# The first unit's splits, squares and measures in another order, a second bank for the given states, and identity products between the first turns

## The chip, the cores and the metric

The kernel runs on one core of a Trainium2 chip, in one launch. The metric is the device time of a launch in microseconds (us), lower is better; the kernel before has a median of 2393.8 us over three runs.

## The reference

One inference step of a decoder with two trunk layers, for a prompt of 2048 tokens and 8 given sequences with 4 new tokens each (32 sample tokens), width 1024. Layer 0 has four HGRN2 heads (A, 128 wide) and four forgetting-attention heads (B, with a paged cache), layer 1 four GLA heads (C, keys 128, values 256). Cut to what matters here:

```python
def even_mixer(h, ...):                    # h = rmsnorm(x, norm_even)
    qa, fa, ia, ga, qb, kb, vb, gb, fb = _split(h @ w_in, ...)
    f = lb + (1.0 - lb) * sigmoid(fa)
    o_a, s_a = gated_linear_chunked(ha(qa), ha(1 - f), ha(ia), ha(log(f)), hgrn_s0)
    ...
def gated_linear_chunked(q, k, v, log_f, s0):          # per chunk, also for the given states s0
    S_new = S * exp(b_last)[..., None] + einsum('bshk,bshv->bhkv', k * exp(b_last - b), v)
```

Layer 1 uses the same recurrence with values twice as wide.

## The kernel before

**Halves, units, turns.** The prompt goes through in two halves of 1024 tokens; the 32 sample tokens ride with the first half (`T` = 1056 columns there). `norm_groups` takes the half's tokens in groups of two tiles of 128 rows (the last group is the 32 sample rows). A group's `prep` loads its rows (`get_tile`, tiles nx_0, nx_128, ...), squares them on ScalarE with a row sum (L421), takes the root (VectorE L403, GpSimd L405) and scales them on VectorE (L423). Its `turn` transposes the rows on TensorE (tiles nt, two PSUM banks in turn) and evacuates each bank twice (`split_evac`): the high half of a two-term float16 on ScalarE (L465), the remainder on VectorE (L466).

**Weight units.** The projections come in units of 256 columns. `half_unit` gives four steps of a unit: 0 fetch (DMA, tile wr), 1 measure (VectorE: four maxima of a 128x512 part each, L292, and their maximum, L294, tile rm), 2 scale (a power of two from that maximum: TensorE spreads it over the partitions by an fp32 product with the identity, tiles spr, L279; VectorE L281, L270 to L272), 3 split (two float16 terms, tile w, in four parts). The parts alternate between two ways to split: scale and high term on ScalarE (L351, L352) with the remainder on GpSimd (L353), or high term on ScalarE (L345) with the remainder on VectorE (L346). Projections then take three matmuls for a k-tile (L470 to L472, high and low terms). The first units are Ai (values of HGRN2, tiles pt_Av; unit 0), Ag (gates, pf_Ag; unit 1) and two of Aqf (queries and forget gates of one head; units 2 and 3). Of the first unit, pS_Av are the sample tokens' projections (L514), for which VectorE copies their columns (sam_Av, L509).

**What sets the order.** Instructions are issued by hand-written generators (`handover`, `staged`, `mux`); `issue_after` sets a point for a block; a scheduler and pools of PSUM banks and tiles place the rest. Each engine takes its instructions in order. `staged` issues the later units' steps beside the running one, by a table `todo` of (unit, step) pairs. The first unit of a run has a table of its own, shown here:

```python
todo = [[(1, 0)], [], [(2, 0)], [(1, 1), (1, 2)], [(1, 3), (3, 0), (2, 1), (2, 2), (2, 3)]]
```

**Given states.** `lin_attn`'s `decode` computes the sample tokens' part of a linear head: for a group of given states sb (name s), TensorE computes keys times values (stS, L687), GpSimd multiplies the state by its decay (L689), VectorE adds the two (L691) and a DMA writes it out. The tile of stS has the PSUM tag "st", which has one bank; "gr" has two, used by transposes and the score products gl. Heads of layer 1 (value width 256) have two such groups in each half of the given states, heads of layer 0 one.

Of the kernel before, what the change touches and what calls it, by code (L numbers as in the profile page):

```python
# [8 lines left out]
F32 = mybir.dt.float32  # L9
# [112 lines left out]
class Kern:  # L122
# [134 lines left out]
    def spread(self, x, pps, tag, nm):  # L257

        nc = self.nc
        m, t = self.kcol(), self.kcol()  # L260
        nc.vector.tensor_reduce(m, x, mybir.AxisListType.X, ALU.max, apply_absolute_value=True)
        ps = pps.tile([P, 512], F32, tag=tag, name=f"spr_{nm}")
        nc.tensor.matmul(ps[:, :P], m.to_broadcast([P, P]), self.ident, start=True, stop=True)
        nc.vector.reduce_max(t, ps[:, :P], axis=mybir.AxisListType.X)
        return t

# [17 lines left out]
    def unit_scale(self, key, parts, rm, pool, pps, nm, undo, k):  # L284

        nc = self.nc

        def measure():
            if key in self.scales:
                return  # L290
            for a, r in enumerate(parts()):
                nc.vector.tensor_reduce(rm()[:, a : a + 1], r, mybir.AxisListType.XY, ALU.max,  # L292
                                        apply_absolute_value=True)
            nc.vector.reduce_max(rm()[:, WSPLIT:], rm()[:, :WSPLIT], axis=mybir.AxisListType.X)  # L294

        def scale():
            if key in self.scales:
                return
            sc = self.scales[key] = self.kcol(3)
            self.power(rm()[:, WSPLIT:], 2.0**14, sc, pool, pps, nm)  # L300
            if undo is not None:
                nc.vector.tensor_scalar(sc[:, 2:3], sc[:, 1:2], undo[:, 1:2], k, ALU.mult, ALU.mult)

        return measure, scale

# [9 lines left out]
    def half_unit(self, pool, pps, w, cols, key, nm, undo=None, k=1.0, also=(), raw=("wr", WU), lean=False):  # L315


        nc = self.nc
# [16 lines left out]
        def split():  # L335
            W = Parts(pool.tile([P, 2, KT, WU], F16, tag="w", name=f"w_{nm}"))
            s = self.scales[key][:, 0:1]
            for dst, inv in also:
                nc.vector.tensor_scalar(dst, self.scales[key][:, 1:2], inv[:, 1:2], None, ALU.mult)
            for a in range(WSPLIT):  # L340
                ks = slice(a * h, (a + 1) * h)
                r = t["raw"][:, ks, :width]
                hi, lo = (x[:, ks, :width] for x in W)
                if a % 2:
                    nc.scalar.activation(hi, r, AF.Copy, scale=s)  # L345
                    nc.vector.scalar_tensor_tensor(lo, r, s, hi, ALU.mult, ALU.subtract)  # L346
                    continue
                if lean:
                    nc.gpsimd.tensor_scalar(r, r, s, None, ALU.mult)
                else:  # L350
                    nc.scalar.activation(r, r, AF.Copy, scale=s)  # L351
                nc.scalar.activation(hi, r, AF.Copy)  # L352
                nc.gpsimd.tensor_tensor(lo, r, hi, ALU.subtract)  # L353
            return W
# [52 lines left out]

    def norm_groups(self, pool, pps, act, hf, get_tile, gain, tags=("gr", "o")):

        nc = self.nc  # L410
        tiles = self.ttiles(hf)

        def mk(grp):
            xs = []

            def prep():
                for c0, n in grp:
                    xt = get_tile(c0, n)
                    sq = pool.tile([P, D], BF16, tag="th", name=f"nsq{c0}")
                    ss = pool.tile([P, 1], F32, tag="nss", name=f"nss{c0}")  # L420
                    nc.scalar.activation(sq[:n], xt[:n], AF.Square, accum_out=ss[:n])  # L421
                    r = self.rstd(pool, ss[:n], [n, 1], D, f"n{c0}")
                    nc.vector.tensor_scalar(xt[:n], xt[:n], r, None, ALU.mult)  # L423
                    xs.append(xt)

            def turn():
                c0 = grp[0][0]
                if grp[-1][0] == HALF:
                    self.sam = None
                for k in range(KT):  # L430
                    ps = pps.tile([P, 512], F32, tag=tags[k % 2], name=f"nt{c0}_{k}")
                    w = 0
                    for (_, n), xn in zip(grp, xs):
                        nc.tensor.transpose(ps[:, w : w + n], xn[:n, k * P : (k + 1) * P], self.ident[:n, :n])
                        w += n
                    self.split_evac(ps[:, :w], act[0][:, k, c0 : c0 + w], act[1][:, k, c0 : c0 + w],
                                    gain[:, k : k + 1])

            return prep, turn

        return [mk(tiles[g : g + 2]) for g in range(0, len(tiles), 2)]

# [59 lines left out]
    def few_rows(self, pps, act, W, c0, nm, width):  # L502
# [3 lines left out]
        if self.sam is None:  # L506
            self.sam = self.few.tile([P, KT, 2, TS], act[0].dtype, tag="sam", name=f"sam_{nm}")
            for j, x in enumerate(act):
                nc.vector.tensor_copy(self.sam[:, :, j], as32(x[:, :, c0 : c0 + TS]))  # L509
# [21 lines left out]
    def lin_attn(self, wp, pps, hf, h, dv, q, f, k, v, vs, sg, gain, S, s0, s_out, p_out, ydst, nm):  # L531
# [107 lines left out]
        def decode():  # L639
# [31 lines left out]
            for half in range(2):  # L671
# [10 lines left out]
                yield 2.4 * dv  # L682
                for x, sb in enumerate(sbs):
                    b0 = 4 * half + x * cpb
                    st = pps.tile([P, cpb, dv], F32, tag="st", name=f"stS_{nm}{b0}")
                    for j in range(cpb):
                        nc.tensor.matmul(st[:, j], kpad[half][:, (b0 + j) % 4], v3, start=True, stop=True)  # L687
                    yield 213 * cpb
# [90 lines left out]
    def even_half(self, hf, act, wpool, wp, pps, npool, S):  # L779
# [7 lines left out]
            return wp.tile([P, HALF + TS], F32, tag="c4", name=nm)  # L787

        def unit(cols, nm, run, k=1.0):
            return (self.half_unit(wpool, pps, w, cols, nm, nm + str(hf), self.sx_even, k), run)  # L790

        def sc(nm):
            return self.scales[nm]
# [155 lines left out]
    def phase_even(self):  # L949
# [4 lines left out]
        with pool("act", side="right") as ap, pool("w", side="right") as w0, pool("wl", side="right") as wp1, \  # L954
# [5 lines left out]
            nrm = Pool(n0, {"th": 1, "nss": 4, "rs_t": 4, "rs_r": 4})  # L960
            self.scales2, self.ready, self.fsc, self.logit, self.v_undo = {}, {}, {}, {}, {}
            self.sx_even = self.gain_scale(self.g_even, pps, "pj", "e")
            S1 = sp.tile([P, P], F32, name="Sx")
            S = [(sp.tile([P, P], F32, name=f"S{h}"), S1) for h in range(NH)]
            act = self.alloc_act(ap)
# [19 lines left out]
            for hf in range(2):  # L985
# [12 lines left out]
                first = self.handover(groups, dense(0, 1), last)  # L998
                if hf == 0:
                    groups[0][0]()  # L1000
                    groups[0] = (lambda: None, groups[0][1])
                    for step in us[0][0]:
                        self.ready[0] = step()
                    drain(first)
                    with tc.issue_after(self.last_x.ins), tc.issue_after(self.last_a.ins), \
                            tc.issue_after(self.last_v.ins):
# [37 lines left out]
    def staged(self, us, a, b, beside=None):  # L1044
# [2 lines left out]

        def step(u, n):
            if u < len(us):
                self.ready[u] = us[u][0][n]()  # L1050

        for j in range(a, b):
            if j:
# [570 lines left out]
    def out_units(self, hf, layer, act, wpool, wp, pps, x2=None, done=None):  # L1624
# [4 lines left out]
        def mk(u):  # L1629
# [3 lines left out]
            def ev(ps, g, cnt, m):  # L1633
# [11 lines left out]
                else:  # L1645
                    for j in range(cnt):
# [4 lines left out]
                        if layer == 0 and u == 3:  # L1651
# [2 lines left out]
            return (self.half_unit(wpool, pps, w, [(u * 256, 256)], f"o{layer}{u}", f"o{layer}{hf}{u}",  # L1654
                                   also=list(zip(undo, (self.sy[layer], self.sy[2]))),
                                   raw=("yr", 256) if (hf, layer, u) == (0, 0, 0) else ("wr", WU),
                                   lean=(hf, layer, u) == (0, 0, 0)),
                    lambda W: self.proj_tm(pps, act, W, hf, ev, f"o{layer}{hf}{u}", pairs=not done or u < 3))

        return [mk(u) for u in range(4)]  # L1660
# [310 lines left out]
```

## Time and profile before

| what | value |
|---|---|
| three runs | 2399.18, 2390.87, 2393.8 us (median 2393.8) |
| profiled execution | 2395.09 us, span 2393.4 us, mean granted TensorE clock 0.987 |
| TensorE busy | 2294.6 us, 96% of the span |
| VectorE, ScalarE, GpSimd busy | 1414.6, 1108.6, 756.9 us |
| DMA | 317.24 MB, 133 GB/s on average |

Times in a row of a timeline are the start from the beginning of the span and the duration, in us; what stands in brackets is the idle time of the engine just before and what ended it. The rows of the list of waits give total, number and longest. A row of a window gives, after the window and its length, the busy time of TensorE, its weight loads, VectorE, ScalarE and GpSimd, the granted clock of TensorE (1 is full), the DMA share and GB/s. Matmuls overlap, so the distance of their starts says what one costs, not its duration. TensorE's `LDWEIGHTS` are counted apart.

### The profile page before, as it was taken

How to read it: one execution, taken by the hardware profiler on the slowest of the kernel's cores; microseconds unless marked ns; L12 is line 12 of the kernel's file. 1: busy time of each engine (PE TensorE's matmuls, PEld its weight loads, DVE VectorE, ACT ScalarE, POOL GpSimd, SP SyncE). 2: the span in 40 equal slices, each digit the busy share in tenths (PEclk: the TensorE clock that was granted, in tenths of full speed). 3: DMA queues.
4: the chain of work that ended last, by engine and by line, in shares of the span. 5: the costliest groups of instructions: out<-in, count | busy, mean ns of one | idle time of the engine just before them, and what ended most of it. 6: DMA issues, size and time to landing. Idle time of an engine off the chain costs nothing. (4 is left out here: it accounts for less than half of the span.)

```text
span 2393.4 us, 58665 instructions
## 1 busy us (share of the span) xinstructions
PE 2294.6 (96%) x23324; PEld 1635.2 (68%) x23324; DVE 1414.6 (59%) x3345; ACT 1108.6 (46%) x2460; POOL 756.9 (32%) x845
## 2 busy tenths in 40 slices
PE   7999999999999999999999999999999999999998
PEld 5667678854655876655446876777778766666887
DVE  7556556546664548567766463654675644557554
ACT  6434243343433126566676454535543635545333
POOL 2233323112212225234456211432452222322223
PEclk9999999999999999999999999999999999999999
DMA  6231235435431276776864632122156312115453
GB/s 182 79 87 58 85 119 161 147 108 148 147 116 59 82 217 214 254 250 200 264 223 155 191 109 63 50 82 85 44 156 193 107 42 69 43 59 159 154 190 150
DMA packets 297012, 317.24 MB, mean 133 GB/s; under 512 B 39729, under 2 KB 241010, under 8 KB 296738
## 3 DMA queue, kind: packets, MB, share of 16 engines
q1 hardware_dynamic: 295234, 308.98, 41.0%
q8 instruction: 183, 3.00, 0.5%
q0 software_dynamic: 1504, 4.52, 0.5%
q14 instruction: 91, 0.75, 0.1%
HBM read 242.31 MB, written 71.11 MB: 131 GB/s over the span
## 5 line engine op out<-in xcount | busy, mean ns | idle before, releaser
L472 PE MATMUL pt_o<-w_o,act 128*128 128x256 f16 x1024 | 280.4, 274 | 3.6 <-DVE act L1603 3.5
L470 PE MATMUL pt_o<-w_o,act 128*128 128x256 f16 x1024 | 280.7, 274 | 0.9 <-ACT sg1C L526 0.9
L471 PE MATMUL pt_o<-w_o,act 128*128 128x256 f16 x1024 | 280.4, 274 | 0.8 <-POOL w_o L353 0.8
L472 PEld LDWEIGHTS <-act 128*128 128x128 f16 x2304 | 226.3, 98 | 35.4 <-DVE act L1603 4.8
L470 PEld LDWEIGHTS <-act 128*128 128x128 f16 x2304 | 226.3, 98 | 35.2 <-ACT act L465 3.2
L471 PEld LDWEIGHTS <-act 128*128 128x128 f16 x2304 | 226.4, 98 | 31.6 <-issue 2.2
L470 PE MATMUL pt_Cv<-w_Cv,act 128*128 128x256 f16 (+1 forms) x512 | 140.4, 275 | 1.8 <-ACT act L465 1.0
L471 PE MATMUL pt_Cv<-w_Cv,act 128*128 128x256 f16 (+1 forms) x512 | 140.3, 275 | 0.0
L636 POOL TENSOR_TENSOR kA<-kA,fA 128x512 f32<-128x512 f32 (+1 forms) x56 | 79.5, 1421 | 191.5 <-PE gl_A L602 141.5
L472 PE MATMUL pt_Cv<-w_Cv,act 128*128 128x256 f16 (+1 forms) x512 | 140.0, 275 | 0.0
L1211 ACT ACTIVATE L<-L,nm,kc 128x512 f32<-128x512 f32 (+3 forms) x160 | 118.2, 741 | 37.8 <-DVE nm L1209 33.5
L636 POOL TENSOR_TENSOR kC<-kC,fC 128x512 f32<-128x512 f32 (+1 forms) x56 | 81.8, 1461 | 151.7 <-PE gl_C L602 107.2
L1219 POOL TENSOR_SCALAR L<-L,nm 128x512 f32<-128x512 f32 (+3 forms) x160 | 98.8, 631 | 63.3 <-DVE nm L1215 22.5
L1246 ACT ACTIVATE th<-pt 128x512 f16<-128x512 f32 (+3 forms) x159 | 80.7, 527 | 64.8 <-PE pt L1239 64.0
L1247 DVE TENSOR_TENSOR tl<-pt,th 128x512 f16<-128x512 f32 (+3 forms) x159 | 94.6, 608 | 23.3 <-ACT th L1246 22.3
L1239 PE MATMUL pt<-ident,L 128*128 128x128 f32 x544 | 92.7, 283 | 5.8 <-POOL L L1219 2.7
L1239 PEld LDWEIGHTS pt<-ident,L 128*128 128x128 f32 x544 | 68.0, 145 | 32.3 <-DVE tl L1247 8.7
L1363 PEld LDWEIGHTS pkt<-ident,pgcache_fox_k 128*128 128x128 f32 x512 | 58.4, 143 | 43.4 <-issue 25.9
L1363 PE MATMUL pkt<-ident,pgcache_fox_k 128*128 128x128 f32 x512 | 76.0, 281 | 7.3 <-DVE kts L1367 5.2
L470 PE MATMUL pt_Av<-w_Ai,act 128*128 128x256 f16 x256 | 70.2, 275 | 1.3 <-ACT act L465 1.3
L471 PE MATMUL pt_Av<-w_Ai,act 128*128 128x256 f16 x256 | 70.3, 275 | 0.8 <-POOL w_Ai L353 0.8
L472 PE MATMUL pt_Bk<-w_Bk,act 128*128 128x256 f16 x256 | 70.6, 276 | 0.0
(952 smaller groups left out, 6744.4 us busy)
## 6 DMA issues: line engine op xcount, KB each, us to landing
pgcache_fox_k<-in_cache_fox_k SPq DMA_DIRECT2D x128, 256.0 KB, 4.3
pgcache_fox_v<-in_cache_fox_v SPq DMA_DIRECT2D x128, 256.0 KB, 4.0
yr<-yT SPq DMA_DIRECT2D x16, 1024.0 KB, 6.6
nx<-in_x_prompt SPq DMA_DIRECT2D x16, 512.0 KB, 4.7
wr_Aqf<-in_w_in_even SPq DMA_DIRECT2D x64, 128.0 KB, 3.4
wr_o<-in_w_out_even SPq DMA_DIRECT2D x32, 256.0 KB, 4.2
wr_Cv<-in_w_in_odd SPq DMA_DIRECT2D x32, 256.0 KB, 4.1
wr_Cqk<-in_w_in_odd SPq DMA_DIRECT2D x64, 128.0 KB, 2.9
```

The costliest lines, as they stand in the source:

```text
L470: nc.tensor.matmul(ps, lh[0], rh[0], start=first, stop=False)
L471: nc.tensor.matmul(ps, lh[0], rh[1], start=False, stop=False)
L472: return nc.tensor.matmul(ps, lh[1], rh[0], start=False, stop=last)
L636: nc.gpsimd.tensor_tensor(kv[:, :, 0], kv[:, :, 0], t1.to_broadcast([P, nb, w]), ALU.mult)
L1211: self.last_exp = nc.scalar.activation(lt[:, :w], lt[:, :w], AF.Exp, bias=nm[:, 0:1], scale=ib, accum_out=nm[:, 2 + j : 3 + j])
L1219: nc.gpsimd.tensor_scalar(lt[:, :w], lt[:, :w], nm[:, 1:2], 2.0**14, ALU.mult, ALU.mult)
L1239: nc.tensor.transpose(pt[:, w : w + P], rows[b][s // 4][0][:, (s % 4) * P : (s % 4 + 1) * P], self.ident)
L1246: nc.scalar.activation(th[:, a:w], pt[:, a:w], AF.Copy),
L1247: nc.vector.tensor_tensor(tl[:, a:w], pt[:, a:w], th[:, a:w], ALU.subtract)))
L1363: nc.tensor.transpose(pk[:, j * P : (j + 1) * P], pgs[j][:, h * P : (h + 1) * P], self.ident)
```

## The change

Five parts:

1. The first unit (Ai, first half) splits all four parts as L345 and L346, high term on ScalarE and remainder on VectorE; before, two of four went through L351, L352 and L353. The flag `lean` of `half_unit` becomes `scaler` with the values None, "pool" and "vector".
2. The loads of the groups 1 and 2 of normalised rows are issued ahead; the squares and scalings of group 1 stand behind the last split of the first unit, of group 2 in the midst of group 1's turn, of group 3 behind that turn. Turns 1 and later follow.
3. Between the first turn's transposes TensorE gets 21 matmuls of the identity with itself into a bank (`warm`) that nothing reads: nine behind the first spread, four behind the first transpose, and one behind every transpose of the second tile.
4. The steps beside the first unit follow another table, and the measures of units 1 to 3 are issued after the last evacuation on VectorE at that point (`last_v`; the sample copies set it as well).
5. stS takes "st" and "gr" in turn for the groups of given states of one half.

```diff
-    def half_unit(..., raw=("wr", WU), lean=False):
+    def half_unit(..., raw=("wr", WU), scaler=None):
...
-                if a % 2:
-                    nc.scalar.activation(hi, r, AF.Copy, scale=s)
+                if a % 2 or scaler == "vector":
+                    self.last_split = nc.scalar.activation(hi, r, AF.Copy, scale=s)
                     nc.vector.scalar_tensor_tensor(lo, r, s, hi, ALU.mult, ALU.subtract)
                     continue
-                if lean:
+                if scaler == "pool":
...
+            def load():
+                raw.extend(get_tile(c0, n) for c0, n in grp)
             def prep():
-                for c0, n in grp:
-                    xt = get_tile(c0, n)
+                for j, (c0, n) in enumerate(grp):
+                    xt = raw[j] if raw else get_tile(c0, n)
...
-            def turn():
+            def turn(each=None):
...
+                            self.last_t = nc.tensor.transpose(...)
+                            if each:
+                                each(st, k, j)
...
             for j, x in enumerate(act):
-                nc.vector.tensor_copy(self.sam[:, :, j], as32(x[:, :, c0 : c0 + TS]))
+                self.last_v = nc.vector.tensor_copy(self.sam[:, :, j], as32(x[:, :, c0 : c0 + TS]))
...
-                    st = pps.tile([P, cpb, dv], F32, tag="st", name=f"stS_{nm}{b0}")
+                    st = pps.tile([P, cpb, dv], F32, tag=("st", "gr")[x % 2], name=f"stS_{nm}{b0}")
...
+            warm = pps.tile([P, 512], F32, tag="st", name="warm")
+            def warm_up(n, after):
+                with tc.issue_after(after.ins):
+                    for _ in range(n):
+                        nc.tensor.matmul(warm[:, :P], self.ident, self.ident, start=True, stop=True)
+            warm_up(9, self.last_spread)
...
                 if hf == 0:
                     groups[0][0]()
-                    groups[0] = (lambda: None, groups[0][1])
                     for step in us[0][0]:
                         self.ready[0] = step()
+                    for g in groups[1:3]:
+                        g[2]()
+                    def behind(ins, g):
+                        with tc.issue_after(ins.ins):
+                            groups[g][0]()
+                    def each0(st, k, j):
+                        if j or k == 0:
+                            warm_up(1 if j else 4, self.last_t)
+                        if (k, j) == (2, 0):
+                            st.enter_context(tc.issue_after(self.last_scale.ins))
+                    def turn0():
+                        groups[0][1](each0)
+                    def turn1():
+                        groups[1][1](lambda st, k, j: behind(self.last_a, 2) if (k, j) == (KT // 2, 0) else None)
+                        behind(self.last_a, 3)
+                    steps = [lambda: None, lambda: behind(self.last_split, 1), lambda: None, lambda: None, groups[4][0]]
+                    turns = [turn0, turn1] + [g[1] for g in groups[2:]]
+                    first = self.handover(list(zip(steps, turns)), dense(0, 1), last)
...
                 with ExitStack() as st:
+                    if beside and n == 1 and u < 4:
+                        st.enter_context(self.tc.issue_after(self.last_v.ins))
                     self.ready[u] = us[u][0][n]()
...
-                todo = [[(1, 0)], [], [(2, 0)], [(1, 1), (1, 2)], [(1, 3), (3, 0), (2, 1), (2, 2), (2, 3)]]
+                todo = [[(1, 0)], [(1, 1)], [(2, 0), (1, 2), (1, 3)], [(3, 0)], [(2, 1), (2, 2), (2, 3)]]
```

TensorE and VectorE at the end of the first unit. In the rows pS_Av are the sample tokens' products, spr_Aqf the spread of unit 2's maximum (rm_Aqf_717 before, rm_Aqf_737 after) and pf_Ag unit 1's products. TensorE before, in the midst of the pS_Av:

```order
L514 MATMUL pS_Av_665<-w_Ai_153,sam_Av_662 32x256
L279 MATMUL spr_Aqf_723<-ident,rm_Aqf_717 128x128
L514 LDWEIGHTS sam_Av_662
L514 MATMUL pS_Av_665<-w_Ai_153,sam_Av_662 32x256
L514 LDWEIGHTS sam_Av_662
```

TensorE after, at the end of the pS_Av:

```order
L522 MATMUL pS_Av_705<-w_Ai_163,sam_Av_702 32x256
L522 LDWEIGHTS sam_Av_702
L522 MATMUL pS_Av_705<-w_Ai_163,sam_Av_702 32x256
L279 MATMUL spr_Aqf_743<-ident,rm_Aqf_737 128x128
L478 LDWEIGHTS w_Ag_599
L478 MATMUL pf_Ag_869<-act,w_Ag_599 128x352
```

The spread moved from between the 8th and 9th pS_Av to behind the 24th, directly ahead of the first pf_Ag. VectorE before, where that maximum is taken (nt_7 is the first group's last bank, nt_0 to nt_2 the second group's):

```order
L466 SCALAR_TENSOR_TENSOR act<-nt_7_239,g_even,act 128x256
L292 TENSOR_REDUCE rm_Aqf_717<-wr_Aqf_556 128x1
L466 SCALAR_TENSOR_TENSOR act<-nt_0_264,g_even,act 128x256
L292 TENSOR_REDUCE rm_Aqf_717<-wr_Aqf_556 128x1
L423 TENSOR_SCALAR nx_512_184<-nx_512_184,rsr_n_191 128x1024
L294 TENSOR_REDUCE rm_Ag_648<-rm_Ag_648 128x1
L403 TENSOR_SCALAR rst_n_199<-nss_197 128x1
L292 TENSOR_REDUCE rm_Aqf_717<-wr_Aqf_556 128x1
L466 SCALAR_TENSOR_TENSOR act<-nt_1_269,g_even,act 128x256
L292 TENSOR_REDUCE rm_Aqf_717<-wr_Aqf_556 128x1
L466 SCALAR_TENSOR_TENSOR act<-nt_2_274,g_even,act 128x256
```

VectorE after, from the sample copies on (rm_Aqf_903 is unit 3's maximum, few_Av the sum of the pS_Av):

```order
L292 TENSOR_REDUCE rm_Aqf_737<-wr_Aqf_582 128x1 x4
L165 TENSOR_SCALAR g_hgrn<-g_hgrn 128x4
L165 TENSOR_SCALAR g_gla<-g_gla 128x8
L172 TENSOR_TENSOR lb<-lb 128x4
L191 MEMSET wgr 80x512
L213 CAST mdiag<-ident 128x128
L232 MEMSET scT_855 128x1024
L232 MEMSET scT_856 128x1024
L292 TENSOR_REDUCE rm_Aqf_903<-wr_Aqf_693 128x1 x4
L527 TENSOR_TENSOR few_Av_730<-few_Av_730,pS_Av_705 32x256
L210 CAST mlev_803<-mtmp 128x64
L294 TENSOR_REDUCE rm_Aqf_737<-rm_Aqf_737 128x1
```

The reductions of unit 2's maximum moved behind the two sample copies (the row ahead of these), and its last step L294 behind the memsets and unit 3's reductions.

ScalarE over the second group's evacuations (nsq are squares; the number in nx is the first token). Before:

```order
L465 ACTIVATE act<-nt_0_264,g_even 128x256
L421 ACTIVATE nsq_196,nss_197<-nx_640_194 128x1024
L465 ACTIVATE act<-nt_1_269,g_even 128x256
L465 ACTIVATE act<-nt_2_274,g_even 128x256
L421 ACTIVATE nsq_246,nss_247<-nx_768_244 128x1024
L465 ACTIVATE act<-nt_3_279,g_even 128x256
L465 ACTIVATE act<-nt_4_284,g_even 128x256
L421 ACTIVATE nsq_256,nss_257<-nx_896_254 128x1024
```

After:

```order
L426 ACTIVATE nsq_270,nss_271<-nx_512_176 128x1024
L473 ACTIVATE act<-nt_4_268,g_even 128x256
L473 ACTIVATE act<-nt_5_289,g_even 128x256
L426 ACTIVATE nsq_278,nss_279<-nx_640_178 128x1024
L473 ACTIVATE act<-nt_6_294,g_even 128x256
L473 ACTIVATE act<-nt_7_299,g_even 128x256
L426 ACTIVATE nsq_306,nss_307<-nx_768_304 128x1024
L426 ACTIVATE nsq_316,nss_317<-nx_896_314 128x1024
L426 ACTIVATE nsq_386,nss_387<-nx_1024_384 32x1024
L473 ACTIVATE act<-nt_0_394,g_even 128x256
```

The squares that stood between the second group's evacuations, one after each or two, came to stand later, the last three together ahead of the third group's first evacuation.

TensorE in the first C head's decode. Before, up to stS_C002 (the next pair, stS_C004, comes behind 89 further rows):

```order
L602 MATMUL gl_C_21886<-qC_21136,kC_21137 24x16 x32
L687 MATMUL stS_C_21929<-hl_C_21762,kpad_C_21771 128x256 x2
L471 LDWEIGHTS act
L471 MATMUL pt_Cv_21943<-w_Cv_21226,act 128x256
L472 LDWEIGHTS act
```

After, stS_C002 and stS_C004:

```order
L695 MATMUL stS_C_21949<-hl_C_21782,kpad_C_21791 128x256 x2
L479 LDWEIGHTS act
L479 MATMUL pt_Cv_21963<-w_Cv_21246,act 128x256
L480 LDWEIGHTS act
L480 MATMUL pt_Cv_21963<-w_Cv_21246,act 128x256
L478 LDWEIGHTS act
L478 MATMUL pt_Cv_21963<-w_Cv_21246,act 128x256
L479 LDWEIGHTS act
L479 MATMUL pt_Cv_21963<-w_Cv_21246,act 128x256
L480 LDWEIGHTS act
L480 MATMUL pt_Cv_21963<-w_Cv_21246,act 128x256
L695 MATMUL stS_C_22053<-hl_C_21782,kpad_C_21792 128x256 x2
```

The third pair, stS_C004, moved up to five pt_Cv matmuls behind the second.

More of the change, by code (lines that the diff above doesn't have):

```diff
@@ L262, in spread @@
         ps = pps.tile([P, 512], F32, tag=tag, name=f"spr_{nm}")
-        nc.tensor.matmul(ps[:, :P], m.to_broadcast([P, P]), self.ident, start=True, stop=True)
+        self.last_spread = nc.tensor.matmul(ps[:, :P], m.to_broadcast([P, P]), self.ident, start=True, stop=True)
         nc.vector.reduce_max(t, ps[:, :P], axis=mybir.AxisListType.X)
@@ L301, in scale @@
             if undo is not None:
-                nc.vector.tensor_scalar(sc[:, 2:3], sc[:, 1:2], undo[:, 1:2], k, ALU.mult, ALU.mult)
+                self.last_scale = nc.vector.tensor_scalar(sc[:, 2:3], sc[:, 1:2], undo[:, 1:2], k, ALU.mult, ALU.mult)
         return measure, scale
@@ L313, in sources, with half_unit @@
                 off += n
-    def half_unit(self, pool, pps, w, cols, key, nm, undo=None, k=1.0, also=(), raw=("wr", WU), lean=False):
+    def half_unit(self, pool, pps, w, cols, key, nm, undo=None, k=1.0, also=(), raw=("wr", WU), scaler=None):
         nc = self.nc
@@ L413, in mk @@
         def mk(grp):
-            xs = []
+            xs, raw = [], []
+            def load():
+                raw.extend(get_tile(c0, n) for c0, n in grp)
             def prep():
-                for c0, n in grp:
-                    xt = get_tile(c0, n)
+                for j, (c0, n) in enumerate(grp):
+                    xt = raw[j] if raw else get_tile(c0, n)
                     sq = pool.tile([P, D], BF16, tag="th", name=f"nsq{c0}")
@@ L429, in turn @@
                     self.sam = None
[L430 to L439, printed above, removed]
+                with ExitStack() as st:
+                    for k in range(KT):
+                        ps = pps.tile([P, 512], F32, tag=tags[k % 2], name=f"nt{c0}_{k}")
+                        w = 0
+                        for j, ((_, n), xn) in enumerate(zip(grp, xs)):
+                            self.last_t = nc.tensor.transpose(ps[:, w : w + n], xn[:n, k * P : (k + 1) * P], self.ident[:n, :n])
+                            w += n
+                            if each:
+                                each(st, k, j)
+                        self.split_evac(ps[:, :w], act[0][:, k, c0 : c0 + w], act[1][:, k, c0 : c0 + w],
+                                        gain[:, k : k + 1])
+            return prep, turn, load
         return [mk(tiles[g : g + 2]) for g in range(0, len(tiles), 2)]
@@ L789, in unit @@
         def unit(cols, nm, run, k=1.0):
-            return (self.half_unit(wpool, pps, w, cols, nm, nm + str(hf), self.sx_even, k), run)
+            return (self.half_unit(wpool, pps, w, cols, nm, nm + str(hf), self.sx_even, k,
+                                   scaler="vector" if (hf, nm) == (0, "Ai0") else None), run)
         def sc(nm):
@@ L1049, in step @@
             if u < len(us):
-                self.ready[u] = us[u][0][n]()
+                with ExitStack() as st:
+                    if beside and n == 1 and u < 4:
+                        st.enter_context(self.tc.issue_after(self.last_v.ins))
+                    self.ready[u] = us[u][0][n]()
         for j in range(a, b):
@@ L1656, in mk @@
                                    raw=("yr", 256) if (hf, layer, u) == (0, 0, 0) else ("wr", WU),
-                                   lean=(hf, layer, u) == (0, 0, 0)),
+                                   scaler="pool" if (hf, layer, u) == (0, 0, 0) else None),
                     lambda W: self.proj_tm(pps, act, W, hf, ev, f"o{layer}{hf}{u}", pairs=not done or u < 3))
```

## The prediction

> **What bounds the kernel now.** I read the page's busy shares first, then the waits of TensorE in the first 70 us and where the added bank acts, then the timelines of those places. The page:
>
> ```profile
> PE 2294.6 (96%) x23324; PEld 1635.2 (68%) x23324; DVE 1414.6 (59%) x3345; ACT 1108.6 (46%) x2460; POOL 756.9 (32%) x845
> PE   7999999999999999999999999999999999999998
> ```
>
> TensorE is busy for 96% of the span, with the first 60-us slice among its two emptiest. So work taken off VectorE, ScalarE or GpSimd is worth something only where TensorE stands still for it. TensorE's waits from 0 to 70 us, and behind the dots one row from 1500 to 1800 us (total, times, longest):
>
> ```profile
> PE nt L434 <- DVE nx L423: 5.5, 3, 3.7
> ...
> PE nt L434 <- DVE act L466: 2.8, 2, 2.2
> PE pf_Ag L470 <- ACT w_Ag L352: 1.5, 1, 1.5
> PE pS_Av L514 <- DVE sam_Av L509: 1.2, 1, 1.2
> PE pt_Av L471 <- POOL w_Ai L353: 0.8, 1, 0.8
> PE pf_Ag L470 <- DVE pow_Aqf L281: 0.8, 1, 0.8
> ...
> PE stS_C L687 <- DVE s_C L691: 6.5, 3, 2.2
> ```
>
> The change touches a start with some 13 us of waits in the rows shown and three waits of 2.2 us later. TensorE's timeline (start, duration):
>
> ```profile
> 19.80 0.39 PE L470 MATMUL pt_Av<-w_Ai,act 128*128 128x256 f16 x1
> 21.03 0.37 PE L471 MATMUL pt_Av<-w_Ai,act 128*128 128x256 f16 x1 [0.84 <-POOL w_Ai L353]
> ...
> 23.12 0.42 PE L470 MATMUL pt_Av<-w_Ai,act 128*128 128x256 f16 x1
> 23.33 0.42 PE L471 MATMUL pt_Av<-w_Ai,act 128*128 128x256 f16 x1
> ...
> 24.42 0.27 PE L472 MATMUL pt_Av<-w_Ai,act 128*128 128x256 f16 x1
> 24.53 0.27 PE L470 MATMUL pt_Av<-w_Ai,act 128*128 128x256 f16 x1
> ...
> 49.80 0.27 PE L472 MATMUL pt_Av<-w_Ai,act 128*128 128x256 f16 x1
> ...
> 51.93 0.49 PE L279 MATMUL spr_Aqf<-ident,rm_Aqf 128*128 128x128 f32 x2
> 52.34 0.62 PE L514 MATMUL pS_Av<-w_Ai,sam_Av 128*32 128x256 f16 x16
> 54.49 0.47 PE L470 MATMUL pf_Ag<-act,w_Ag 128*128 128x352 f16 x1 [1.53 <-ACT w_Ag L352]
> 56.08 0.45 PE L470 MATMUL pf_Ag<-act,w_Ag 128*128 128x352 f16 x1 [0.81 <-DVE pow_Aqf L281]
> ...
> 60.72 0.50 PE L471 MATMUL pf_Ag<-act,w_Ag 128*128 128x352 f16 x1
> 61.02 0.46 PE L472 MATMUL pf_Ag<-act,w_Ag 128*128 128x352 f16 x1
> 61.31 0.31 PE L470 MATMUL pf_Ag<-act,w_Ag 128*128 128x352 f16 x1
> 61.46 0.31 PE L471 MATMUL pf_Ag<-act,w_Ag 128*128 128x352 f16 x1
> ```
>
> Starts are 0.21 us apart at 23 us and 0.11 apart at 24.5: the matmuls ran at half clock at first. After the stops around 53 to 56 us the wider pf_Ag matmuls are 0.29 us apart until 61.31, then 0.15. VectorE beside it:
>
> ```profile
> 45.81 2.46 DVE L292 TENSOR_REDUCE rm_Aqf<-wr_Aqf 128x1 f32<-128x512 f32 x4
> ...
> 51.32 0.22 DVE L509 COPY sam_Av<-act 128x256 f16<-128x256 f16 x1
> ...
> 51.67 0.22 DVE L509 COPY sam_Av<-act 128x256 f16<-128x256 f16 x1
> 51.94 0.48 DVE L191 MEMSET wgr<- 80x512 f32 x1
> ...
> 53.74 0.91 DVE L232 MEMSET scT<- 128x1024 f32 x1 [0.16 <-issue]
> 54.57 0.10 DVE L173 TENSOR_TENSOR lb<-lb 128x4 f32<-128x4 f32 x1
> ...
> 58.13 0.41 DVE L519 TENSOR_TENSOR few_Av<-few_Av,pS_Av 32x256 f32<-32x256 f32 x1
> ```
>
> **The change, part by part.** Three terms carry the sum.
>
> *A, the first unit (start to the last pt_Av).* Removed: two scale activations on ScalarE and two subtractions on GpSimd; added: two combined multiply-subtracts on VectorE. The last split then no longer ends behind GpSimd's 0.84 us wait. With squares 256 and 384 out of the way, I put the first pt_Av about 3 us before the 21.03 at which the dense run starts. The identity products keep TensorE active among the first transposes; if they bring full clock before pt_Av, the some 13 matmuls up to 23.7 save 0.1 us each, 1.4 us. Together 4.5 us. The nine products stand where TensorE waited 3.7 us for nx anyway, and the other twelve stand between transposes whose evacuations set the pace; I cost them at nothing, and without that cover they would cost at most their own time, about 3 us for the nine.
>
> Against it stands the new order. ScalarE now runs five squares among and behind the evacuations of the second group and ahead of the third's, the last three without a break:
>
> ```profile
> 22.60 1.10 ACT L421 ACTIVATE nsq<-nx 128x1024 bf16<-128x1024 f32 x1
> 23.55 0.24 ACT L421 ACTIVATION_READ_ACCUMULATOR nsq<-nx 128x1 f32 x1
> ```
>
> A square with its read takes some 1.05 us, so three hold ScalarE for 3.1 us in which no bank is emptied, and a run of four L292 reductions (2.46 us) now stands among the fourth group's evacuations on VectorE. The two sum to 5.6 us, partly beside matmuls, against 4.5 won. I take A = 0, with ends -4.5 (all kept) and +1.5 (all of the 5.6 shows and 4.1 is won).
>
> *B, behind the first unit.* The measure of the third unit moves behind the sample copies. TensorE's queue then has spr_Aqf directly ahead of pf_Ag; before, its operand had been reduced half a unit earlier and it ran among the pS_Av matmuls without a wait. TensorE cannot pass it. VectorE does after the copies: four reductions 2.46, three small L165 and L172 rows 0.2 (they stood between the two copies), the memsets and the cast 2.63 (51.94 to 54.57), four more reductions 2.46, one few_Av add 0.35, and a cast and the final small reduction 0.1 each, like the small row L173: 8.3 us. From 51.89, the end of the copies before, that gives 60.2; spr_Aqf takes 0.5 (its row), so pf_Ag starts near 60.7. The pS_Av matmuls end at 52.96: a hole of over 7 us in place of 1.53 and 0.81.
>
> The gate's split of ScalarE and GpSimd now comes ahead of the copies, so those two waits vanish; nothing else covers the hole. Before, 20 pf_Ag matmuls had started by 61.31 and the other 28 of the 48 take 28 x 0.15 = 4.2: end 65.5. After, from 60.7, with half clock for 3.4 us (12 matmuls, then 36 x 0.15 = 5.4) they end at 69.5; with 6.8 us (23, then 25 x 0.15 = 3.8) at 71.3. So +4.0 to +5.8. The third unit's own split is next: its scale follows spr_Aqf behind four more reductions, so it may be late by up to 1 us. I take B = +5, with ends +3.5 (0.5 us of the chain hidden) and +7.
>
> The sizes 3.4 and 6.8 come from one row, whose eighth figure is the granted clock:
>
> ```profile
> 54.00:55.00 1.00, 0.51 (x2) 0.28 (x3) 1.00 (x3) 1.00 (x3) 0.48 (x1) 0.74 0.22 60
> ```
>
> A mean of 0.74 between full and half puts the switch near 54.5, and 54.5 to 61.31 is 6.8 us at half clock, with the second stop of 0.81 in it. A restart without a second stop may be shorter; I set half of 6.8 as its lower end. The Trainium skill, "TensorE: Matmul & The Clock Gate", section "The HAM clock gate", has a free-running window of about 3.4 us, of which one idle one halves the clock and one busy one restores it. By that rule a hole of 7 us always restarts cold, and the wait before full clock lies between one and two windows, which is what the two ends above are. The trace's 6.8 us are two such windows, so it agrees.
>
> *C, the second bank.* In layer 1 of the first half stS_C002 waits because its bank is read by the add of stS_C000:
>
> ```profile
> 1509.18 0.71 PE L602 MATMUL gl_C<-qC,kC 128*24 128x16 f32 x64
> 1512.07 0.79 PE L687 MATMUL stS_C<-hl_C,kpad_C 96*128 96x256 f32 x2 [2.19 <-DVE s_C L691]
> 1512.67 0.44 PE L471 MATMUL pt_Cv<-w_Cv,act 128*128 128x256 f16 x1
> ...
> 1510.03 1.27 DVE L708 TENSOR_TENSOR vp_C<-vC,vp_C 128x256 fp32r<-128x256 f32 x1
> 1511.33 0.69 DVE L691 TENSOR_TENSOR s_C<-s_C,stS_C 128x512 f32<-128x512 f32 x1
> ```
>
> With the other bank it does not wait, but in the new order stS_C004 follows only five matmuls later and needs the first bank, so the same add at 1511.33. The wait is then entered after stS_C002 (0.6) and five pt_Cv (0.6 to 1.1): 1.2 to 1.7 us per head stand under the wait instead of behind it. Three heads give -3.6 to -5. Part of it may go back where the later heads' work now meets its own operands. I take C = -2, nearer to nothing than to the full sum, since VectorE's order ahead of L691 has not become shorter; ends -6.5 (all three waits) and 0.
>
> The scheduler also shifts rows in the forgetting-attention part of layer 0 and nothing is added there; I take 0, with 2 us either way, the size of one wait of the kind seen above.
>
> Sum: 0 + 5 - 2 = +3 on the profiled 2395.1, so 2398. That execution lies 1.3 us above the median of the three runs, 2393.8; for a median I say 2397.
>
> **Rivals.** *A holds (faster).* If the evacuations behind the three squares are covered by the first group's 48 matmuls, all of A = -4.5 stays; with B at its low end +3.5 and C at -6.5 that is -7.5, 2386. The stretch from 25 to 50 us (busy time of TensorE, its loads, VectorE, ScalarE and GpSimd):
>
> ```profile
> 25.00:50.00 25.00, 24.93 (x220) 21.42 (x217) 18.25 (x49) 14.45 (x35) 3.87 (x6) 1.00 0.49 108
> ```
>
> For it: TensorE was the only engine without slack there, so 10 us of ScalarE could take the squares. Against: all three ends are needed at once, since from +3 it takes 10 us to a verdict of faster.
>
> *The hole costs more (slower).* One mechanism: TensorE stands for spr_Aqf, restarts at half clock for two steps, and finds the third unit's split late behind the four reductions that follow. B is then +7; if the C wait only moves (C = 0) and A is +1, the sum is +8, 2402. It decides when the end of the 48 pf_Ag moves past 72 us.
>
> *The second bank does not help.* stS_C004 takes over the whole wait, C = 0: 2399. This and the next stay within the bound.
>
> *The hole is not there*, because spr_Aqf's operand is reduced in time: B = -2, and the total is about -4, 2390. Against it stands the order of VectorE's queue.
>
> **How the numbers follow.** About 0.3%, 7.2 us, is what this kernel's runs can tell from no change. The forecast with C between its ends 0.45; second bank worthless 0.15; hole absent 0.06; the slower rival 0.24; the faster one 0.10. The first three are within the bound, but for a few hundredths at its edge; so faster 0.10, same 0.64, slower 0.26. The range 2389 to 2406 leaves out the full gain of A with C, and a hole that sets off further waits.
>
> **What would show it.** Right: the first pt_Av before 19 us with a short spacing; the last pt_Av again near 49 to 51 us; a wait of 6 to 7 us at spr_Aqf for L294 and pf_Ag matmuls 0.29 us apart behind it; the two waits of pf_Ag gone; the three waits of 2.2 us at stS_C about half as long and at stS_C004. Wrong: a last pt_Av near 45 us, a wait at spr_Aqf below 3 us, or half clock behind it for more than 7 us.

## The result

| kernel | runs | median | lowest to highest | to the kernel before |
|---|---|---|---|---|
| before | 6 | 2396.49 us | 2390.87 to 2399.99 | 1 |
| changed | 6 | 2407.39 us | 2405.05 to 2410.52 | 1.0052, 95% interval 1.0039 to 1.0065 |

The change makes the kernel slower by 0.52%, some 12 us (9 to 16 by the interval). The forecast was 2397 us, a change within 0.3%, with 2389 to 2406 as range: the time lies above it. The profiled execution of the changed kernel took 2405.05 us, and its page begins:

```profile
span 2403.3 us, 58746 instructions
...
PE 2295.2 (96%) x23366; PEld 1636.0 (68%) x23366; DVE 1421.3 (59%) x3347; ACT 1109.0 (46%) x2458; POOL 754.7 (31%) x843
```

TensorE's busy time differs from before by 0.6 us, the span by 9.9: the loss is standing still. Where it arises is found by pairing TensorE's matmuls of the two traces by output and count:

| matmul | before, us | changed, us | difference |
|---|---|---|---|
| pt_Av, 1st | 19.80 | 14.43 | -5.4 |
| pt_Av, 49th (second group) | 28.78 | 23.17 | -5.6 |
| pt_Av, 145th (fourth group) | 43.05 | 43.28 | +0.2 |
| pS_Av, 9th | 52.34 | 52.70 | +0.4 |
| pf_Ag, 17th | 60.14 | 65.01 | +4.9 |
| pt_Bk, 52nd | 368.15 | 370.31 | +2.2 |
| fo, 472nd (forgetting attention) | 1300.06 | 1298.50 | -1.6 |
| pt_o, 105th (output projection, layer 0) | 1319.21 | 1320.66 | +1.5 |
| pt_o, 205th | 1331.03 | 1340.50 | +9.5 |
| pf_C03q, 67th (fourth C head) | 1707.32 | 1718.12 | +10.8 |
| end of the span | 2393.4 | 2403.3 | +9.9 |

There are two jumps: 4.5 us at pf_Ag, which was forecast, and some 9 us between the 97th pt_o (1318.33 us before, difference -0.5) and the 219th (1333.47 us before, +8.7), at a place that the prediction never looked at. The slower drift between the two can't be read from single traces: before, e10 and e13 (below) have the same order on every engine up to 1315 us, and their 472nd fo start at 1300.06, 1294.33 and 1300.57 us. So only jumps within a short stretch are read here, or many traces together.

TensorE's waits up to 80 us, changed kernel:

```profile
PE spr_Aqf L279 <- DVE kc L261: 7.2, 1, 7.2
PE spr_e L263 <- DVE kc L261: 3.4, 1, 3.4
PE nt L440 <- DVE act L474: 1.9, 2, 1.2
PE pS_Av L522 <- DVE sam_Av L517: 1.7, 2, 1.5
PE pt_Av L478 <- ACT act L473: 0.9, 1, 0.9
PE nt L440 <- DVE nx L428: 0.7, 2, 0.4
```

The pf_Ag waits of before are gone and one of 7.2 us stands in their place (L261 is the row behind L294, and the two overlap at 60.4 to 60.5; in e1 and e9 the same wait is put down to rm_Aqf L294). The timelines of TensorE and, behind the dots, VectorE:

```profile
52.70 0.62 PE L522 MATMUL pS_Av<-w_Ai,sam_Av 128*32 128x256 f16 x16 [0.22 <-DVE sam_Av L517]
60.56 0.79 PE L279 MATMUL spr_Aqf<-ident,rm_Aqf 128*128 128x128 f32 x2 [7.24 <-DVE kc L261]
61.15 0.50 PE L478 MATMUL pf_Ag<-act,w_Ag 128*128 128x352 f16 x1
...
64.08 0.35 PE L479 MATMUL pf_Ag<-act,w_Ag 128*128 128x352 f16 x1
64.27 0.31 PE L480 MATMUL pf_Ag<-act,w_Ag 128*128 128x352 f16 x1
...
52.15 2.45 DVE L292 TENSOR_REDUCE rm_Aqf<-wr_Aqf 128x1 f32<-128x512 f32 x4
...
57.51 2.39 DVE L292 TENSOR_REDUCE rm_Aqf<-wr_Aqf 128x1 f32<-128x512 f32 x4
59.93 0.41 DVE L527 TENSOR_TENSOR few_Av<-few_Av,pS_Av 32x256 f32<-32x256 f32 x1
60.27 0.17 DVE L210 CAST mlev<-mtmp 128x64 int8<-128x64 f32 x1
60.37 0.14 DVE L294 TENSOR_REDUCE rm_Aqf<-rm_Aqf 128x1 f32<-128x4 f32 x1
```

From 52.15 to 60.37 VectorE runs the chain of the prediction, 8.2 us, and the pf_Ag matmuls start 0.29 us apart, half clock, from 61.15 to 64.1.

At the output projection TensorE waits (1300 to 1430 us, changed kernel; before had no wait for w_o L352 or sam_o here):

```profile
PE pt_o L478 <- ACT w_o L352: 3.9, 1, 3.9
PE pS_o L522 <- DVE sam_o L517: 1.7, 2, 1.5
...
PE pt_o L480 <- POOL act L1645: 0.8, 1, 0.8
PE pt_o L478 <- ACT act L1644: 0.8, 1, 0.8
...
PE pt_o L479 <- POOL w_o L353: 0.6, 1, 0.6
```

ScalarE and SyncE's queue say why. The first four rows are ScalarE and SyncE before, the next three ScalarE and SyncE of the changed kernel; yr is a piece of y on its way to `act` (four of 256 columns and a last one of 32), row are the residual rows:

```profile
1318.28 0.72 ACT L1602 ACTIVATE act<-yr,kc 128x512 f16<-128x512 f32 x1 [4.78 <-DMA yr<-yT]
...
1320.74 0.33 ACT L1602 ACTIVATE act<-yr,kc 128x64 f16<-128x64 f32 x1
...
1309.95 5.76 SPq L1589 DMA_DIRECT2D yr<-yT  x2
1315.82 5.82 SPq L1833 DMA_DIRECT2D row<-in_x_prompt  x8
...
1330.35 0.35 ACT L1647 ACTIVATE act<-yr,kc 128x64 f16<-128x64 f32 x1 [5.06 <-DMA yr<-yT]
...
1314.68 3.44 SPq L1878 DMA_DIRECT2D row<-in_x_prompt  x6
1321.74 0.38 SPq L1634 DMA_DIRECT2D yr<-yT  x1
```

The last piece is split 9.6 us later than before. Before, ScalarE stood 4.78 us for the piece ahead of it and not at all for this one; now it stands 5.06 us for this one, with the splits of the next unit's w_o behind it in its queue, and those are what TensorE waits for. The order of SyncE's queue tells it without a time: before, all yr pieces stood ahead of the nine rows; now the 32-column piece stands behind six.

```
before:   yr[128x8x256] yr[128x8x32] row_0 row_1 row_2 row_3 row_4 row_5 row_6 row_7 row_8
changed:  yr[128x8x256] row_0 row_1 row_2 row_3 row_4 row_5 yr[128x8x32] row_6 row_7 row_8
```

The edit contains nothing of this place. The scheduler that lays out the whole program came to another choice there; why it did is not shown.

### The profile page after: what moved, and what is told of

The parts are those of the page before. It is cut to its first block, busy times and chain, and to the rows that moved or that the text cites. A ratio compares the mean times of both kernels' runs of the same rounds, so it can differ in the third digit from the quotient of the medians.

```text
span 2403.3 us, 58746 instructions
## 1 busy us (share of the span) xinstructions
PE 2295.2 (96%) x23366; PEld 1636.0 (68%) x23366; DVE 1421.3 (59%) x3347; ACT 1109.0 (46%) x2458; POOL 754.7 (31%) x843
## 5 line engine op out<-in xcount | busy, mean ns | idle before, releaser
L1291 ACT ACTIVATE th<-pt 128x512 f16<-128x512 f32 (+3 forms) x159 | 81.0, 528 | 60.5 <-PE pt L1284 58.4
L478 PE MATMUL pt_Av<-w_Ai,act 128*128 128x256 f16 x256 | 70.6, 276 | 2.1 <-ACT act L473 2.1
L479 PE MATMUL pt_Av<-w_Ai,act 128*128 128x256 f16 x256 | 70.6, 276 | 0.6 <-DVE w_Ai L346 0.6
L480 PE MATMUL pt_Av<-w_Ai,act 128*128 128x256 f16 x256 | 70.5, 276 | 0.3 <-DVE act L474 0.2
```

Source lines behind the costliest of these rows:

```text
L478: nc.tensor.matmul(ps, lh[0], rh[0], start=first, stop=False)
L479: nc.tensor.matmul(ps, lh[0], rh[1], start=False, stop=False)
L480: return nc.tensor.matmul(ps, lh[1], rh[0], start=False, stop=last)
L1291: nc.scalar.activation(th[:, a:w], pt[:, a:w], AF.Copy),
```

## Experiments

Two theories were set against each other. Q: that one load's place in SyncE's queue costs most of the loss. H: the hole at spr_Aqf, with its restart, costs it all. Runs came in four lots with the kernel before beside them, whose medians were 2393.0 to 2393.7 us, so ratios are compared, not medians.

**e1**, the split undone: in `unit`, `scaler=None` for Ai0. By the order, this alone puts the short piece ahead again.

```diff
-    scaler="vector" if (hf, nm) == (0, "Ai0") else None
+    scaler=None
```

> The changed kernel, with the first unit split as before (two of four parts by ScalarE and GpSimd). VectorE's late maximum and with it the 7 us hole at spr_Aqf stays; in SyncE's queue the load of the last 32 columns of y (yr, 128x8x32) stands again ahead of all nine row loads of the output projection. Theory Q (queue: some 8 us of the 11 come from that load standing behind six row loads): 2396 to 2402 us, against 2407 for the changed kernel; the second jump near 1320 to 1330 us is gone, the hole of 7 us is there. Theory H (hole: the restart behind spr_Aqf carries the whole loss): 2405 to 2409.

Measured: 2398.39 us, ratio 1.0019 (1.0008 to 1.0030). The wait at spr_Aqf is 7.2 us as in the changed kernel, no wait for w_o stands at 1300 to 1345 us. Theory H, that the hole costs it all, falls.

**e2**, the measures freed:

```diff
-                    if beside and n == 1 and u < 4:
-                        st.enter_context(self.tc.issue_after(self.last_v.ins))
```

> The changed kernel, without the rule that puts the measures of units 1 to 3 behind the last evacuation. spr_Aqf stands among the pS_Av again, and SyncE's queue has the old order at the output projection. Theory Q: 2390 to 2396, both losses gone, by 11 to 17 us under the changed kernel. Theory H: the same, since the hole is gone as well. It bounds what the rest of the change is worth; no wait over 2 us at spr_Aqf.

Measured: 2396.31 us, ratio 1.0005 (0.9991 to 1.0019): no hole, no late piece, and no gain either.

**e3**, both edits:

> The changed kernel with both edits: split as before, measures without the rule. No hole at spr_Aqf, but SyncE's queue has the short load of y behind six row loads, as the changed kernel has. Theory Q: 2400 to 2406, a jump of 6 to 10 us near 1320 to 1340. Theory H: 2390 to 2397.

Measured: 2399.50 us, ratio 1.0033 (1.0019 to 1.0047). No hole, but the late piece, and slower than before; the time lies between the ranges of the two theories, at the edge of Q's.

**e4**, the kernel before with the vector split alone (`if a % 2 or vec:`, `vec` for Ai0 of the first half):

> The kernel before, with one part of the change alone: the first unit's four parts split by ScalarE and VectorE. No hole at spr_Aqf; SyncE's queue has the short load of y behind six row loads. Theory Q: 2400 to 2406, slower than before by 4 to 10 us though the start is not slower. Theory H: 2394 to 2397, within 1 us of the kernel before.

Measured: 2397.35 us, ratio 1.0020 (1.0006 to 1.0035): less than Q expected, and just above H's range. In its trace the third pf_Ag starts at 51.60 us (56.08 before), 4.5 us ahead; the 219th pt_o at 1342.26 (1333.47), 8.8 us behind. So the start is ahead with these splits, and the jump at the load that moves with them is larger than that. What the splits alone would be worth in the time is not shown: in e6, with rows held back, they win nothing over e10.

**e5**, the changed kernel with every row load of both output projections held behind the last load of y:

```diff
+                self.last_yr = nc.sync.dma_start(t["raw"], y[...])
...
+                    with self.tc.issue_after(self.last_yr.ins):
                         nc.sync.dma_start(t[:m], self.rows(hf, c0, m, first))
```

> The changed kernel, in which the nine row loads of the output projection are issued only after the last load of y, so that the 32-column piece stands ahead of them in SyncE's queue; the start with its hole is as in the changed kernel. Theory Q (the piece behind six row loads costs some 6 to 8 us): 2398 to 2402 us, 5 to 9 us below the changed kernel, and w_o's wait of 3.9 us on TensorE is gone. Theory R (the loss there comes from the other shifted rows of ScalarE and GpSimd, not from this load): 2405 to 2409. The state loads s_C move ahead of the piece too; if these hold it up, the wait stays under Q as well.

Measured: 2394.57 us, ratio 0.9998 (0.9984 to 1.0011), better than Q said. Against the changed kernel its trace gains 6 us between 1316 and 1474 us, and over 10 us from 2200 us on, where the same edit holds back rows of layer 1's last projection. The edit did two things, so e9 and e10 take them apart.

**e6**, e4 with the same edit:

> The kernel before, with the vector split of the first unit alone, and the row loads behind the last load of y. No hole and no late piece. Theory Q: 2389 to 2394, 4 to 8 us below the vector split alone (2397.4) and perhaps faster than the kernel before, since that run's trace was 4.5 us ahead of before at 56 us. Theory R: 2396 to 2399.

Measured: 2388.00 us, ratio 0.9973 (0.9963 to 0.9984), a little below Q's range, with the same double effect as e5.

**e7** and **e8**, the second bank added to before, and taken from the changed kernel (`tag=("st", "gr")[x % 2]` against `tag="st"`):

> The kernel before with the second bank for stS alone. The forecast had -2 us; the trace of the changed kernel shows stS_C004 3 to 4 us earlier in each head and the next head's products back where they were. Theory G (given back): 2392 to 2396, within 1 us of before. Theory C (the wait was worth 1.2 to 1.7 us per head): 2389 to 2391.

> The changed kernel with one bank for stS as before; the hole and the late piece stay. Theory G: within 1 us of the changed kernel, 2405 to 2408. Theory C: 2 to 5 us slower, 2409 to 2413.

Measured: e7 2390.02 us, ratio 0.9982 (0.9973 to 0.9990); e8 2407.51 us, ratio 1.0051 (1.0033 to 1.0069). So alone it looks worth 4 us, in the changed kernel nothing. TensorE in e7, waits of 1500 to 1800 us and two rows:

```profile
PE gl_C L602 <- issue: 4.1, 3, 1.5
PE stS_C L687 <- DVE s_C L691: 3.6, 3, 1.2
...
1513.24 0.51 PE L687 MATMUL stS_C<-hl_C,kpad_C 96*128 96x256 f32 x2 [1.21 <-DVE s_C L691]
...
1527.24 0.69 PE L602 MATMUL gl_C<-qC,kC 128*64 128x64 f32 x16 [1.21 <-issue]
```

The wait of 2.19 became 1.21 at stS_C004, as forecast, and another of 1.21 us came at the next gl_C of each head: 6.5 us of three waits became 3.6 and 4.1. Over the whole stretch of these heads, from the first oS_C (1502 us before) to the 40th pf_C03k (1720 us), e7 takes 215.4 us and before 218.0, so 2.6 us are won there, though the two spans are the same (2393.4); the changed kernel takes 216.9 and e8 216.1, so there nothing is won.

**e9**, e5's edit at the first output projection alone:

> The changed kernel, in which only the first output projection's row loads (layer 0, first half) wait in the order for the last load of y; the run before also held the row loads of layer 1's last projection back, whose trace gained 6 us after 2300 us. Theory Q (the late piece alone cost 6 to 8 us): 2398 to 2402 us. Theory L (the gain of the run before came from the last projection alone): 2404 to 2408.

Measured: 2401.51 us, ratio 1.0030 (1.0016 to 1.0044): 0.0022, 5 us, below the changed kernel. In the trace the wait for w_o is gone, and a new one of 3.1 us for the rows, now late themselves, has come; so the edit takes away only a part of the loss there.

**e10**, the edit in the kernel before, where it moves rows of the last projection only:

> The kernel before with the row loads behind the last load of y; in SyncE's queue the first projection keeps its order and only layer 1's last projection changes. Theory L': its row loads stood ahead of the loads of y there and cost 5 to 6 us: 2387 to 2390. If the gain in the trace was chance of that run: 2392 to 2396.

Measured: 2384.63 us, ratio 0.9963 (0.9951 to 0.9975). That is a gain of 9 us, more than expected, beside the question and of the same kind: rows that stood among the loads of y. From 2190 us on the waits before were, first three rows, and in e10, last row:

```profile
PE pt_o L472 <- DVE act L1603: 3.5, 2, 2.5
PE gl_C L602 <- DVE sam_o L509: 2.0, 1, 2.0
PE pt_o L470 <- ACT sg1C L526: 0.9, 1, 0.9
...
PE gl_C L602 <- DVE qC L635: 1.2, 1, 1.2
```

**e11**, e6 with the second bank:

> The kernel before with three edits: vector split of the first unit, row loads behind the last load of y, second bank for stS. No hole, no late piece. From 2388.0 for the first two and -3.4 for the bank alone: 2384 to 2386 if the bank's gain adds, 2387 to 2389 if it is given back as in the changed kernel.

Measured: 2386.45 us, ratio 0.9971 (0.9958 to 0.9985): the bank adds nothing to e6.

**e12**, the changed kernel without the 21 identity products; by the order the short piece is ahead again:

> The changed kernel without the 21 identity products. The hole stays, SyncE's queue has the old order. If they warm the clock: matmuls of the first unit start 0.2 us apart instead of 0.11 for some 15 matmuls, 1.4 us later at the first group's end, though the later waits for evacuations may take it back; time as with the split undone, 2396 to 2401. If they do nothing, the first pt_Av are 0.11 us apart here as well.

Measured: 2394.53 us, ratio 1.0004 (0.9992 to 1.0016), less than expected. The hole of 7.2 us is there and the jump at 1330 us is not. The first unit's matmuls, e12 and, behind the dots, the changed kernel:

```profile
17.14 0.42 PE L480 MATMUL pt_Av<-w_Ai,act 128*128 128x256 f16 x1
17.36 0.42 PE L478 MATMUL pt_Av<-w_Ai,act 128*128 128x256 f16 x1
...
17.13 0.27 PE L480 MATMUL pt_Av<-w_Ai,act 128*128 128x256 f16 x1
17.24 0.27 PE L478 MATMUL pt_Av<-w_Ai,act 128*128 128x256 f16 x1
```

The products do bring full clock early, and 2.3 us at the 46th pt_Av. By the 95th it is -1.0 us: there this execution of the changed kernel has lost its clock again. Even where it has not, in the traces of e5 and e8 (same start), the ninth pS_Av comes at 51.97 and 51.64 us, and in e12 at 51.52: at the end of the unit nothing is left of the products' gain.

**e13**, the clean one: the kernel before with the short piece's load placed behind the sixth row (its steps are issued in the loop over the rows, after `issue_after` of row 5). TensorE's and GpSimd's order is that of before, SyncE's differs in this load alone, and a few rows of ScalarE and VectorE follow it.

> The kernel before with one load moved: the 32-column piece of y is issued behind the sixth row load of layer 0's output projection, as the changed kernel has it; TensorE's and GpSimd's order is that of before, row for row, and the start is untouched. Theory Q: 2398 to 2403 us, with pt_o waiting 3.5 to 4 us for w_o near 1330 us and some 8 us lost there. Theory R (the load is a bystander, the other shifted rows cost the time): 2392 to 2395.

Measured: 2401.33 us, ratio 1.0027 (1.0012 to 1.0042), 6.5 us slower. ScalarE, SyncE, the window of the DMA engines (its last two figures are their busy share and GB/s) and TensorE:

```profile
1329.14 0.35 ACT L1602 ACTIVATE act<-yr,kc 128x64 f16<-128x64 f32 x1 [5.07 <-DMA yr<-yT]
...
1312.97 4.18 SPq L1835 DMA_DIRECT2D row<-in_x_prompt  x6
1317.68 0.38 SPq L1589 DMA_DIRECT2D yr<-yT  x1
...
1318.00:1329.00 11.00, 11.00 (x104) 9.85 (x102) 4.23 (x8) 3.60 (x6) 2.27 (x2) 1.00 1.05 380
...
PE pt_o L470 <- ACT w_o L352: 4.0, 1, 4.0
PE pt_o L471 <- POOL w_o L353: 0.6, 1, 0.6
```

The load is issued some 2 us later than in before, but its split starts 8.4 us later: six rows of 512 KB, 3.1 MB, go through the full DMA engines ahead of its 128 KB, and at 380 GB/s they take 8.3 us. In the trace they land in the order of their issue, some 1.25 us apart (first, second, fourth and fifth at 1321.7, 1322.9, 1325.4 and 1326.7 us), and the piece follows them, as in the changed kernel, where the sixth row lands at 1329.4 us and the piece at 1330.3. TensorE's difference to before goes from 1.3 us at the 500th fo (1305.50) to 8.8 us at the 219th pt_o (1333.47).

**e14**, e10 with the second bank:

> The kernel before with the row loads behind the last load of y (alone 2384.6 us) and the second bank for stS (alone 2390.0, 3.4 below before). If both add: 2380 to 2383; if the bank's gain was chance of that chip or is given back: 2384 to 2387.

Measured: 2384.09 us, ratio 0.9964 (0.9953 to 0.9976). It beats before and the changed kernel, by the row loads; the bank adds nothing that these times can tell.

Set out by the two suspects (ratios to before):

| | short piece ahead | short piece behind six rows |
|---|---|---|
| no hole at spr_Aqf | before 1; e2 1.0005; e7 0.9982 | e13 1.0027; e4 1.0020; e3 1.0033 |
| hole of 7.2 us | e12 1.0004; e1 1.0019 | changed 1.0052; e8 1.0051 |

The right column is above the left in every pairing: 0.0027 (e13 to before), 0.0033 (changed to e1), 0.0048 (changed to e12). The lower row is above the upper unevenly, by 0 (e12 to e2) to 0.0037 (e1 to e7), and other edits differ in these pairs as well.

The traces say the same place by place. From the 500th fo to the 219th pt_o, the five with the short piece behind six rows (changed, e3, e4, e8, e13) take 35.5 to 40.1 us. The seven with it ahead and the rows behind it as before (before, e1, e2, e7, e10, e12, e14) take 28.0 to 28.8, and the four with the rows of this projection held back (e5, e6, e9, e11) 32.4 to 35.1. So the late piece costs some 9 us there on average, 7.5 in the clean pair (e13 to before), and holding the rows back wins back less than half of it. For the hole: the 52nd pt_Bk starts at 369.1 to 377.1 us in the six traces with it (mean 372.7) and at 365.0 to 369.9 in the ten without (mean 367.3); at the 472nd fo the means are 1302.0 and 1297.0. On average, then, some 5 us of the hole last up to 1300 us; e12 is at the low edge, with 369.1 and 1298.3.

## Why the prediction was wrong

The step that failed is the one that gave the rest of the program 0 us with "2 us either way", since "nothing is added there". It dealt with the forgetting-attention part as waits on TensorE and did not follow SyncE's queue into the output projection. What the runs show there is a load of 128 KB that came to stand behind six row loads: 6.5 us by e13 and some 9 us in the traces, over three times the 2 us that were allowed for the place. With it the sum is 9.5 to 12 us, or 11.5 to 14 without C's -2, against the measured 12. No rival named it either: the slower one put the loss at the hole.

Point by point:

- **A = 0, with ends -4.5 and +1.5.** Right in size, +0.4 at pS_Av, but in part by luck: both sides were larger than said. The changed kernel is 7.5 us ahead at the 47th pt_Av (28.57 against 21.06) where 4.5 were forecast, and all of it is taken back by the end of the unit. Rows of that stretch:

```profile
28.55 0.16 DVE L261 TENSOR_REDUCE kc<-g_odd 128x1 f32<-128x8 f32 x1 [1.24 <-DMA g_odd<-in_norm_odd]
...
29.21 0.33 PE L440 MATMUL nt<-ident,nx 128*128 128x128 f32 x1 [1.19 <-DVE act L474]
...
34.31 1.57 ACT L473 ACTIVATE act<-nt,g_even 128x256 f16<-128x256 f32 x4 [3.16 <-PE nt L440]
...
30.00:35.00 5.00, 4.98 (x31) 3.60 (x29) 2.85 (x8) 1.84 (x4) 1.91 (x3) 0.66 0.86 187
```

  The squares held ScalarE as said (24.07 to 31.1, five of them). Not foreseen: a reduction of layer 1's gain waits on VectorE for its DMA in the midst of the evacuations, and TensorE fell back to half clock for part of 30 to 35 us (0.66 granted). In the traces of e5 and e8, with the same start and nearly the same waits of TensorE, that window shows 1.00, so the drop depends on the execution; what sets it off is not shown. It is also not what took the gain back: e5 and e8 are no more than 0.7 us ahead of before at the ninth pS_Av (51.97 and 51.64 against 52.34). From the 47th to the 145th pt_Av before takes 14.5 us, with 32 nt matmuls among them and no stop over 0.15 us; e8 takes 21.3, with 48 nt matmuls and 3.3 us of stops, 2.9 of them for evacuations. So the waits behind the evacuations took back a part, as the prediction has it, and another part of the lead was only transposes put off.
- **B = +5.** Right: 8.2 us of chain against 8.3, the spread at 60.56 against 60.2, half clock for 2.9 us where 3.4 was the lower end, +4.5 us at pf_Ag. The vanished waits vanished. Its 5 us last on average up to 1300 us in the traces, as set out above. The end of single kernels shows less: e12 has the same hole, 3.6 us behind before at 65 us, and ends 0.9 us ahead in its span. How much the hole costs in the time is not settled: between 0 (e12) and about 4 us (e1, at 1.0019).
- **The clock rule.** The Trainium skill, "TensorE: Matmul & The Clock Gate", section "The HAM clock gate", would have a hole of 7 us restart cold, and full clock after one to two windows of 3.4 us. The restart was cold and half clock lasted 2.9 us from the first pf_Ag, 3.5 from spr_Aqf, so it agrees at its short end. In the other five traces with the hole it lasted 2.9 to 5.8 us from spr_Aqf: the cold restart and the size agree, but the shortest (e9) lies below one window.
- **C = -2.** The mechanism was right; the size holds in the traces of the kernel before, not in the changed kernel: over the stretch of the three heads the bank wins 2.6 us (e7 to before), 2.9 (e11 to e6) and 1.5 (e14 to e10), while the changed kernel takes 0.8 longer than e8. stS_C002 goes without a wait and stS_C004 takes 1.2 us of it, but a wait of 1.2 us at gl_C takes the place. Removing the bank from the changed kernel changes nothing (e8), adding it to before gave 4 us over a lot (e7), to e10 and e6 nothing (e14, e11). So 2 us or so may be there in the kernel before; whether e7's 4 us are real is open.

## What to carry over

Where a scheduler lays out the whole program, an edit of its first 60 us can move a DMA 1250 us later: compare the order of every queue over the whole program, SyncE's above all, and price each load that changes places with larger ones by the bytes put ahead of it over the bandwidth there. When a part of a change seems to cost or win, see whether its variants fall into the same order at such a place; four unrelated edits here (the split, the identity products, the measures, a forced order) flipped the same load. And loads that only a later stage needs are better held behind the small ones that a running stage waits for: that alone was worth 9 us at the last projection of the kernel before. It has its own price where the running stage soon needs those loads too: at the first projection, e9 left a wait of 3.1 us for the rows.

## What was not expected of the hardware

A load of 128 KB took 11.5 us from its issue (1317.68) to the instruction that waited for it (1329.14), with the DMA engines full at 380 GB/s and 3.1 MB issued ahead of it; before, with nothing of its queue just ahead but another piece, the same load landed 3.4 us after its issue (1315.35 to 1318.8). And products that nothing reads set the clock: with 21 of them from 3.95 us on, nine ahead of the first transpose, the first projection's matmuls started 0.11 us apart at 17 us; without them 0.21, up to 19.5 us, although the transposes were the same. That this is the clock is read from the distances alone: the granted clock of both traces shows 1.00 from 10 to 20 us, though e12 runs at the distance that goes with a clock of one half at 30 to 33 us in the changed kernel.
